# fox_rwkv7_hybrid_block on one core: the first branch weight cast on GpSimd, gate loads ahead of weight loads, modulation products singly between output products

## The chip, the cores and the metric

The kernel runs on one core of a Trainium2 chip. The metric is the device time of one execution in microseconds (us); the median of several runs is compared. One further execution was profiled, and every row of a profile comes from that one.

Engines go by the names of the profile: PE is TensorE's products and PEld its weight loads, DVE is VectorE, ACT is ScalarE, POOL is GpSimd, SP is SyncE. SPq is SP's queue, from which nearly all DMAs are issued, one behind the other.

## The reference

One block of a hybrid model over 1024 tokens of width 1024, all in float32. What is computed, cut to what matters:

```python
mod = silu(c) @ w_mod + b_mod
shift1, scale1, gate1, shift2, scale2, gate2 = split(mod, 6)
u = modulate(rms_norm(h, ln1_g), shift1, scale1)       # xn * (1 + scale) + shift
proj = u @ w_in                                         # fox columns, rwkv columns, gate columns
o_fox = fox_attention(q, k, v, log_sigmoid(f + b_f))    # 8 heads of 64
o_rwkv = rwkv7_time_mix(p_rwkv, ...)                    # 8 heads of 64
gate_fox, gate_rwkv = split(sigmoid(p_gate), 2)
merged = gate_fox * (o_fox @ fox_w_out) + gate_rwkv * (o_rwkv @ rwkv_w_out)
h = h + gate1 * (merged @ w_o)
u = modulate(rms_norm(h, ln2_g), shift2, scale2)
a, b = split(u @ w_up, 2)                               # 2816 columns each
h = h + gate2 * ((silu(conv(a)) * b) @ w_down)
out = rms_norm(h, final_g)
```

The change touches the products `o_fox @ fox_w_out` and `o_rwkv @ rwkv_w_out` (the branch products), `merged @ w_o` (the output product), and the two pieces shift2 and scale2 of `mod`.

## The kernel before

A float32 product is made of three products: each operand is split into a high part, rounded to the format that TensorE takes at full pace, and a low part, the remainder; high by high, low by high and high by low are summed in PSUM. A cast makes the high part, a subtraction the low part.

The order of TensorE's instructions is written out by hand. That of the other engines is, up to the middle of the output product, set by a scheduler that sees what each instruction needs, and by extra order edges (`add_manual_dep` with `NOSYNC`): such an edge says that one instruction stands behind another in the order, and adds no wait.

**Branch products.** `br_part(x, n, hf)` makes one part: branch x (0 attention, 1 RWKV), column tile n (0 to 7), token half hf. It has 12 products of 128x512 into one PSUM bank. 32 parts follow one another, in the order (0,0,0), (0,1,0), (0,0,1), (0,1,1), and then (x,n,0), (x,n,1) for each further n. They take banks 1 to 4 in turn, so that a part starts when VectorE has emptied the bank of the fourth part before it. VectorE does that with the multiplication by the gate: `mg = g * ps` for x = 0 (L1306), `g = g * ps` and `mg = mg + g` for x = 1 (L1308, L1309).

`br_open(x, n)` prepares a column tile. The raw weight `raw_br` is loaded by `br_load` (L1206, two buffers), ScalarE casts it into `hi_br` (L1214), GpSimd subtracts for `lo_br` (L1215), and the gate tile `g` is read back from DRAM (L1217, two buffers). Tile n+1 is opened, and the weight of tile n+2 loaded, ahead of the parts of tile n.

In the same stage run `mod_steps` (the loads `wm` of `w_mod`, L1267, and VectorE's sums over them into `acc`, for segments 3 and 4), `rk_make` (the RWKV operands: load `rk_raw`, ScalarE's cast, VectorE's subtraction, both into `rk_m` tiles, L1293 and L1294), `wo_load` (the weights of the output product) and `mg_split` (the split of the merged operand, tiles `mgh_f` and `mgl`). The work of the stage before ends beside the first parts: `fx` are the attention's operands, `tp` its transposes, `rk_ps` the last gate columns, `rest` their sigmoid.

**Output product.** `wo_mm(t, kt, ps)` makes six products of 128x512 for token tile t and contraction step kt. The loop goes over kt for t = 0 and 1, and from kt = 5 on steps of t = 2 follow. At kt == 4 the generator `mod_2` runs through: for each of the two segments eight fp32 products of a 128x128 piece of `acc` with a column of ones, into one column each of a PSUM tile `mps`; then VectorE adds the bias.

Of the kernel before, what the change touches and what calls it, by code (L numbers as in the profile page):

```python
# [17 lines left out]
KT = 8  # L18
NH = 512
# [16 lines left out]
NOSYNC = mybir.DependencyInfo(mybir.DependencyClass.NoSync, mybir.DependencyReason.DATA)  # L36
# [96 lines left out]
def hybrid_block(ctx: ExitStack, tc: tile.TileContext, a, out):  # L133
    nc = tc.nc
# [3 lines left out]
    def mm(o, lhsT, rhs, start, stop, more=False):  # L138

        weave.mm_cost(o, lhsT, rhs)  # L140
        nc.tensor.matmul(o, lhsT, rhs, start=start, stop=stop, skip_group_check=more)  # L141
# [5 lines left out]
    def f32(ap):  # L147
        return ap.bitcast(F32)
# [17 lines left out]
    def V(name, i=0, n=1):  # L166
        o, _ = VEC[name]
        return vec[:, o + i : o + i + n]
# [34 lines left out]
    d_gate = dr.tile([16, 128, S], F32, name="d_gate")  # L203
# [25 lines left out]
    def mod_part_steps(acc, ps, seg, dst):  # L229
        for j in range(KT):  # L230
            mm(ps[:, j : j + 1], acc[:, j * 128 : j * 128 + 128], ones[:, 0:1], start=True, stop=True)
            yield
        nc.vector.tensor_tensor(dst, ps[:, 0:KT], V("b_mod", seg * 8, KT), op=ALU.add)
# [10 lines left out]
    marks = {}  # L244
# [101 lines left out]
    with ExitStack() as es:  # L346
# [66 lines left out]
        with tc.tile_pool(name="st", bufs=1) as st, tc.tile_pool(name="stp", bufs=2, space=PS) as stp, \  # L413
# [126 lines left out]
            for half in range(2):  # L540
                for kt in u_steps(half):
                    low_part(kt, half, (0, 1))
                    if half == 0 and kt in (3, 5):
                        raw, hi, lo = low_raw[kt == 5]
# [465 lines left out]
    with tc.manual_schedule(engines={mybir.EngineType.DVE, mybir.EngineType.Activation}):  # L1010
# [6 lines left out]
        def slot(free):  # L1017
            while not free:
                yield 100
            yield free.popleft() - weave.now  # L1020
# [165 lines left out]
    def bank(k, name):  # L1186
        return pb.tile([128, NH], F32, tag="big", name=name) if k > 5 else pz.tile([128, NH], F32, tag=f"p{k}", name=name)
# [11 lines left out]
    br = br_st.enter_context(tc.tile_pool(name="br", bufs=2, reuse_waits="tile"))  # L1199
    opened = {}  # L1200

    br_raw = {}

    def br_load(x, n):
        raw = br_raw[x, n] = rp.tile([128, 1024], F32, tag="raw", name=f"raw_br{x}{n}")[:, 0:NH]
        nc.sync.dma_start(raw, a["w_br"][n, :, x * NH : x * NH + NH])  # L1206

    def br_open(x, n):
        if (x, n) not in br_raw:
            br_load(x, n)  # L1210
        raw = br_raw[x, n]
        hi = br.tile([128, NH], F32R, tag="whi", name=f"hi_br{x}{n}")
        lo = br.tile([128, NH], F32R, tag="wlo", name=f"lo_br{x}{n}")
        marks["br"] = nc.scalar.copy(hi, raw)  # L1214
        nc.gpsimd.tensor_tensor(lo, raw, f32(hi), op=ALU.subtract)  # L1215
        g = br.tile([128, S], F32, tag="g", name=f"g{x}_{n}")
        nc.sync.dma_start(g, d_gate[8 * x + n])  # L1217
        opened[x, n] = (hi, lo), g

    br_open(0, 0)  # L1220
    br_open(0, 1)
    if "rest" in marks:
        g, m = (gsp.tile([128, NH], F32, tag="sp0", name=f"rest{k}") for k in range(2))
        i = nc.scalar.activation(g, marks["rest"], AF.Abs)
# [36 lines left out]
    def mod_steps():  # L1261

        for seg in (3, 4):
            acc = slot(f"e{seg - 1}", f"acc{seg}")
            for kt in range(KT):
                w = slot(f"a{4 + kt % 4}", f"wm{seg}_{kt}")
                i = nc.sync.dma_start(w, a["w_mod"][kt * 128 : kt * 128 + 128, seg * D : seg * D + D])  # L1267
                if "i" in last:
                    tc.add_manual_dep(i.ins, last["i"].ins.name, NOSYNC)
                if kt == 0:  # L1270
                    ts(acc, w, sc[:, 0:1], None, op0=ALU.mult)
                else:
                    stt(acc, w, sc[:, kt : kt + 1], acc, op0=ALU.mult, op1=ALU.add)
                yield
            accs.append(acc)
# [8 lines left out]
    def mg_split(hf, n):  # L1284
        split(mg_hl[hf][0][n], mg_hl[hf][1][n], mg[hf][n])
# [24 lines left out]


    mods = mod_steps()
    for x in range(2):
        for n in range(8):
            if x or n:
                k = 8 * x + n + 1
                if k < 16:
                    br_open(k // 8, k % 8)
                if k < 15:
                    br_load((k + 1) // 8, (k + 1) % 8)  # L1320
            parts = [(x, n, 0), (x, n, 1)]
            if x == 0 and n < 2:
                parts = [(0, 0, 0), (0, 1, 0)] if n == 0 else [(0, 0, 1), (0, 1, 1)]
            for _ in range(0 if x and n > 3 else 1 if x else 2 if n < 6 else 0):
                next(mods, None)
            for part in parts:
                br_part(*part)
            if x == 0 and 1 <= n <= 4:
                rk_make((n - 1) // 2 * 2, (n - 1) % 2)
            if x == 1:  # L1330
                wo_load(n)
                if n == 0:
                    lo = [hp.tile([128, NH], F32R, tag=tag, name=f"mgl0_{k}", bufs=bufs)
                          for k, (tag, bufs) in enumerate(5 * [("xq", 5)] + 2 * [("s", 2)] + [("dg", 1)])]
                    mg_hl[0] = pairs([f"f{k}" for k in range(4)], "mgh0"), lo
                else:
                    mg_split(0, n - 1)
# [46 lines left out]
        h_sb[t] = slot(f"m{(4 if t < 4 else 8) + t}", f"h_sb{t}")  # L1384
        nc.sync.dma_start(h_sb[t], a["x"][t * 128 : t * 128 + 128, :])

    def wo_mm(t, kt, ps):
        hf, rows = t // 4, slice(t % 4 * 128, t % 4 * 128 + 128)
        x, w = [p[kt] for p in mg_hl[hf]], wo[kt]
        for c in range(2):  # L1390
            for n, (xi, wi) in enumerate(PARTS):
                mm(ps[c], x[xi][:, rows], w[wi][:, c * NH : c * NH + NH], start=kt == 0 and n == 0, stop=kt == KT - 1 and n == 2)

    def wo_row(t, ps):

        for c in range(2):
            cs = slice(c * NH, c * NH + NH)
            x, h = row_tmp[2 * t + c] if t < 5 else hp.tile([128, NH], F32, tag=("dg", "xq")[c], name=f"wo{t}_{c}", bufs=(1, 5)[c]), h_sb[t][:, cs]
            tt(x, ps[c], g1b[:, cs], op=ALU.mult)
            tt(h, h, x, op=ALU.add)  # L1400
            nc.scalar.activation(x, h, AF.Square, accum_out=ssq[:, 8 * c + t : 8 * c + t + 1])
        nc.sync.dma_start(d_h[t], h_sb[t])
# [213 lines left out]
    def mod_2():  # L1616
        for i, acc in enumerate(accs):
            yield from mod_part_steps(acc, bank(3 + i, f"mps{3 + i}"), 3 + i, m2[:, i * 8 : i * 8 + 8])
        stt(A2, m2[:, 8:16], 1.0, V("ln2_g", 0, 8), op0=ALU.add, op1=ALU.mult)
# [9 lines left out]

    ps = {t: [bank(k, f"wo{t}_{c}") for c, k in enumerate(ks)] for t, ks in enumerate(((0, 5), (6, 7), (1, 2)))}  # L1630
    behind = {5: (0, 1, 2, 3), 6: (4, 5), 7: (6, 7)}
    for kt in range(KT):
        for t in range(2):
            wo_mm(t, kt, ps[t])
        mg_split(1, kt)
        if kt == 4:
            for _ in mod_2():
                pass
        for k in behind.get(kt, ()):
            wo_mm(2, k, ps[2])  # L1640
    for t in range(3):
        wo_row(t, ps[t])
    def wo_do(t, k):
        ps = [bank(k + c, f"wo{t}_{c}") for c in range(2)]
        for kt in range(KT):
            wo_mm(t, kt, ps)
        return ps

    ps = wo_do(3, 3)
# [7 lines left out]
    ps = wo_do(4, 0)  # L1657
# [15 lines left out]
    for t, k in ((5, 2), (6, 6), (7, 4)):  # L1673
        ps = wo_do(t, k)
# [229 lines left out]
    for s, k in enumerate(ORDER):  # L1904
        ps = banks[4:] if k in (7, 4, 2) else banks[0:4]
# [109 lines left out]
```

## Time and profile before

| | |
|---|---|
| median of 3 runs | 1658.31 us (1658.08 to 1660.62) |
| the profiled execution's own time | 1662.01 us |
| span in its profile | 1660.2 us |
| mean granted TensorE clock | 0.989 |
| PE, PEld | 97%, 81% of the span |
| DVE, ACT, POOL | 74%, 50%, 8% |

The span is what the profile sees from the first instruction to the last; the execution's own time holds a little more. A share is an average over the whole span, and stages differ. The branch products lie at about 829 to 919 us, the output product behind them. In a row of the timeline stand start, length, engine, line, operation, output<-input and count, and in brackets the engine's idle time ahead of it and what ended that. L141 is the helper through which every product goes, so the tile's name tells products apart.

### The profile page before, as it was taken

What the parts mean: (1) busy time and instruction counts of PE and PEld (TensorE: products, weight loads), DVE (VectorE), ACT (ScalarE), POOL (GpSimd) and SP (SyncE); (2) the same over time, 40 slices, a digit from 0 to 9 for tenths busy, and PEclk for the clock granted to TensorE, in tenths of its full rate; (3) what the DMA queues carried; (4) which work ended last, traced back from release to release, by engine and by line L of the source; (5) the groups of instructions that cost most, each with busy time, mean ns of one, the idle gap of its engine ahead of it and who ended that gap; (6) DMA issues with size and microseconds to landing.
All of it is one profiled execution on the core that took longest, in us unless ns stands there. A gap on an engine that the chain in (4) does not pass through costs nothing.

```text
span 1660.2 us, 25947 instructions
## 1 busy us (share of the span) xinstructions
PE 1615.2 (97%) x9694; PEld 1346.1 (81%) x9694; DVE 1223.2 (74%) x2371; ACT 822.3 (50%) x1540; POOL 130.3 (8%) x152
## 2 busy tenths in 40 slices
PE   7999999999999999999999999999999999999998
PEld 7777777898978788888778887888888888888886
DVE  5786787878876536888678347897777777786677
ACT  5563335444455656666623225654444444555455
POOL 0011001111111011221022000000000000000000
PEclk9999999999999999999999999999999999999999
DMA  8488645443343246433187411243223223574363
GB/s 336 139 322 238 177 116 140 131 121 97 100 115 97 96 129 153 124 114 110 64 323 265 166 70 58 66 138 108 96 95 120 97 96 108 208 266 156 125 209 108
DMA packets 121645, 240.59 MB, mean 145 GB/s; under 512 B 40048, under 2 KB 48880, under 8 KB 121520
## 3 DMA queue, kind: packets, MB, share of 16 engines
q1 hardware_dynamic: 113040, 220.58, 40.7%
q0 software_dynamic: 8480, 18.37, 4.2%
q8 instruction: 76, 1.25, 0.3%
q14 instruction: 49, 0.40, 0.1%
HBM read 173.35 MB, written 65.54 MB: 144 GB/s over the span
## 4 chain that ended last, share of the span: by engine, by line
PE 62%; DVE 3%; ACT 2%; DMA 1%; issue 1%; SPq 0%; ACTq 0%; DVEq 0%
PE X L141 14%; PE D L141 13%; PE Y L141 7%; PE wo L141 5%; PE br L141 5%; PE gt L141 4%; PE rk_ps L141 4%; PE W L141 3%; PE lg L141 2%; PE ov L141 2%; PE tp L145 2%; DVE nm L1049 1%; DVE P L1059 1%; DMA g<-d_gate 0%; DVE tl L1089 0%
## 5 line engine op out<-in xcount | busy, mean ns | idle before, releaser
L141 PE MATMUL D<-op,op 128*128 128x512 f32 x924 | 209.8, 389 | 0.0
L141 PEld LDWEIGHTS D<-op,op 128*128 128x128 f32 x924 | 173.3, 188 | 36.3 <-DVE op L1252 0.3
L141 PE MATMUL X<-T_m,S 128*128 128x512 f32 x440 | 106.9, 389 | 0.0
L141 PEld LDWEIGHTS X<-T_m,S 128*128 128x128 f32 x440 | 82.5, 188 | 17.5 <-ACT x L1542 0.4
L1251 ACT CAST op<-g 128x512 fp32r<-128x512 f32 x77 | 47.8, 621 | 72.1 <-PE D L141 47.8
L1252 DVE TENSOR_TENSOR op<-g,op 128x512 fp32r<-128x512 f32 x77 | 53.0, 688 | 41.1 <-ACT op L1251 41.1
L1502 DVE SCALAR_TENSOR_TENSOR c<-ab,vec,c 128x512 f32<-128x512 f32 x88 | 65.9, 749 | 18.4 <-ACT c L1505 16.8
L784 DVE TENSOR_TENSOR t<-E,M 128x60 f32<-128x60 f32 (+24 forms) x248 | 56.1, 226 | 26.6 <-DMA M<-sm 20.6
L274 DVE TENSOR_TENSOR lo_in<-raw_in,hi_in 128x512 fp32r<-128x512 f32 x84 | 57.7, 725 | 22.0 <-PE gt L141 7.2
L1466 DVE TENSOR_TENSOR A<-ur,A 128x512 fp32r<-128x512 f32 x64 | 43.9, 688 | 39.0 <-ACT A L1462 38.8
L1466 DVE TENSOR_TENSOR S<-ur,S 128x512 fp32r<-128x512 f32 x66 | 45.5, 691 | 35.2 <-ACT S L1462 35.1
L1462 ACT CAST S<-ur 128x512 fp32r<-128x512 f32 x66 | 41.0, 622 | 56.1 <-DVE ur L1455 30.9
L141 PE MATMUL Y<-T_h,S 128*128 128x512 f32 x264 | 65.6, 398 | 1.6 <-ACT T_h L1720 1.0
L141 PE MATMUL Y<-T_h,A 128*128 128x512 f32 x264 | 63.4, 389 | 0.0
L1053 ACT ACTIVATE P<-lg,nm 128x896 f32<-128x896 f32 (+3 forms) x64 | 47.4, 742 | 29.3 <-DVE nm L1049 19.6
L141 PEld LDWEIGHTS Y<-T_h,S 128*128 128x128 f32 x264 | 50.6, 192 | 13.4 <-ACT T_h L1720 1.8
L1462 ACT CAST A<-ur 128x512 fp32r<-128x512 f32 x64 | 39.6, 621 | 42.9 <-PE X L141 31.0
L141 PE MATMUL W<-B_f,A 128*128 128x512 f32 x252 | 60.6, 389 | 0.0
L786 DVE TENSOR_TENSOR E<-E,t 128x60 f32<-128x60 f32 (+24 forms) x248 | 55.8, 225 | 6.4
L141 PE MATMUL X<-B_b,A 128*128 128x512 f32 x252 | 60.5, 389 | 0.0
L141 PEld LDWEIGHTS Y<-T_h,A 128*128 128x128 f32 x264 | 49.5, 188 | 10.3
L272 ACT CAST hi_in<-raw_in 128x1024 fp32r<-128x1024 f32 x42 | 43.9, 1049 | 25.4 <-PE ps_rkv L141 11.3
(481 smaller groups left out, 4142.0 us busy)
## 6 DMA issues: line engine op xcount, KB each, us to landing
raw_in<-in_w_in SPq DMA_DIRECT2D x50, 512.0 KB, 3.9
wm<-in_w_mod SPq DMA_DIRECT2D x48, 512.0 KB, 6.7
ur<-in_w_up SPq DMA_DIRECT2D x44, 512.0 KB, 4.0
g<-d_g SPq DMA_DIRECT2D x35, 512.0 KB, 3.8
d_g<-gs SPq DMA_DIRECT2D x44, 256.0 KB, 2.0
d_g<-c SPq DMA_DIRECT2D x33, 256.0 KB, 4.3
d_st<-qh SPq DMA_DIRECT2D x64, 128.0 KB, 2.4
stA<-d_st POOLq DMA_DIRECT2D x8, 1024.0 KB, 6.2
```

What stands on the lines that cost most here:

```text
L141: nc.tensor.matmul(o, lhsT, rhs, start=start, stop=stop, skip_group_check=more)
L145: nc.tensor.transpose(o, i, eye)
L272: nc.scalar.copy(hi, raw)
L274: nc.vector.tensor_tensor(lo[:, c : c + NH], raw[:, c : c + NH], f32(hi[:, c : c + NH]), op=ALU.subtract)
L784: tt(tv, E32[:, 0:J, s : s + 1].to_broadcast([128, J, W]), M32[:, s : s + 1, s + 1 : 32].to_broadcast([128, J, W]), op=ALU.mult)
L786: tt(E32[:, 0:J, s + 1 : 32], E32[:, 0:J, s + 1 : 32], tv, op=ALU.add)
L1053: nc.scalar.activation(e[:, 0:n], lg[:, 0:n], AF.Exp, bias=nm[:, 0:1], accum_out=nm[:, 1:2])
L1251: nc.scalar.copy(hi, src)
L1252: tt(lo, src, f32(hi), op=ALU.subtract)
L1462: nc.scalar.copy(hi, src)
L1466: tt(lo, src, f32(hi), op=ALU.subtract)
L1502: stt(c, ab[:, x + hf * NH : x + hf * NH + NH], V("conv_w", 22 * x + i), c, op0=ALU.mult, op1=ALU.add)
```

## The change

It has three parts.

1. The cast of the first weight (x = 0, n = 0) is done by GpSimd instead of ScalarE.
2. Each weight load of the branch products and each load `wm` gets an order edge to the gate load that was written last ahead of it in the code.
3. `wo_mm` takes a generator and draws one modulation product from it after every second product, for t = 0 and 1 from kt = 4 on; what is left is drawn at the last kt.

```diff
+    def after_gate(i):
+        if "g" in marks:
+            tc.add_manual_dep(i.ins, marks["g"].ins.name, NOSYNC)
+
     def br_load(x, n):
         raw = br_raw[x, n] = rp.tile([128, 1024], F32, tag="raw", name=f"raw_br{x}{n}")[:, 0:NH]
-        nc.sync.dma_start(raw, a["w_br"][n, :, x * NH : x * NH + NH])
+        after_gate(nc.sync.dma_start(raw, a["w_br"][n, :, x * NH : x * NH + NH]))
...
-        marks["br"] = nc.scalar.copy(hi, raw)
+        if x or n:
+            marks["br"] = nc.scalar.copy(hi, raw)
+        else:
+            nc.gpsimd.tensor_copy(hi, raw)
         nc.gpsimd.tensor_tensor(lo, raw, f32(hi), op=ALU.subtract)
         g = br.tile([128, S], F32, tag="g", name=f"g{x}_{n}")
-        nc.sync.dma_start(g, d_gate[8 * x + n])
+        marks["g"] = nc.sync.dma_start(g, d_gate[8 * x + n])
...
                 i = nc.sync.dma_start(w, a["w_mod"][kt * 128 : kt * 128 + 128, seg * D : seg * D + D])
+                after_gate(i)
...
-    def wo_mm(t, kt, ps):
+    def wo_mm(t, kt, ps, between=iter(())):
...
                 mm(ps[c], x[xi][:, rows], w[wi][:, c * NH : c * NH + NH], start=kt == 0 and n == 0, stop=kt == KT - 1 and n == 2)
+                if (3 * c + n) % 2:
+                    next(between, None)
...
+    mod2 = mod_2()
     for kt in range(KT):
         for t in range(2):
-            wo_mm(t, kt, ps[t])
+            wo_mm(t, kt, ps[t], mod2 if kt > 3 else iter(()))
         mg_split(1, kt)
-        if kt == 4:
-            for _ in mod_2():
+        if kt == KT - 1:
+            for _ in mod2:
                 pass
```

How this moves instructions shows at three places. The first is SP's queue at the start of the branch stage, before (`raw_br_9238` is the second weight, x = 0 and n = 1; `g_0` and `g_1` are the first two gate tiles; `d_gate<-gs` writes gate columns to DRAM):

```order
L1172 DMA d_gate<-gs_1_8654 128x512
L1206 DMA raw_br_9238<-in_w_br 128x512
L1172 DMA d_gate<-gs_0_8777 128x512
L1172 DMA d_gate<-gs_1_8940 128x512
L1172 DMA d_gate<-gs_0_9097 128x512
L1217 DMA g_0_9236<-d_gate 128x1024
L1217 DMA g_1_9244<-d_gate 128x1024
```

And the same place now:

```order
L1172 DMA d_gate<-gs_1_8654 128x512
L1172 DMA d_gate<-gs_0_8777 128x512
L1172 DMA d_gate<-gs_1_8940 128x512
L1172 DMA d_gate<-gs_0_9097 128x512
L1224 DMA g_0_9236<-d_gate 128x1024
L1210 DMA raw_br_9238<-in_w_br 128x512
L1224 DMA g_1_9244<-d_gate 128x1024
```

The second weight's load has moved behind three writes of gate columns and the first gate load. The second place is SP's queue further on, from the last write of gate columns, before (`raw_br_9372` and `raw_br_9420` are the weights of n = 4 and 5):

```order
L1231 DMA d_gate<-rest_9246 128x512
L1206 DMA raw_br_9372<-in_w_br 128x512
L1206 DMA raw_br_9420<-in_w_br 128x512
L1267 DMA wm_2_9326<-in_w_mod 128x1024
L1267 DMA wm_3_9329<-in_w_mod 128x1024
L1267 DMA wm_4_9374<-in_w_mod 128x1024
L1267 DMA wm_5_9377<-in_w_mod 128x1024
L1217 DMA g_2_9322<-d_gate 128x1024
L1217 DMA g_3_9370<-d_gate 128x1024
```

And now (`raw_br_9324` is the weight of n = 3, which stood ahead of this piece before):

```order
L1238 DMA d_gate<-rest_9246 128x512
L1224 DMA g_2_9322<-d_gate 128x1024
L1210 DMA raw_br_9324<-in_w_br 128x512
L1274 DMA wm_2_9326<-in_w_mod 128x1024
L1274 DMA wm_3_9329<-in_w_mod 128x1024
L1224 DMA g_3_9370<-d_gate 128x1024
L1210 DMA raw_br_9372<-in_w_br 128x512
L1274 DMA wm_4_9374<-in_w_mod 128x1024
L1274 DMA wm_5_9377<-in_w_mod 128x1024
L1224 DMA g_4_9418<-d_gate 128x1024
```

The gate tile of n = 2 has moved ahead of the weights of n = 3 to 5 and of four modulation weights, and from here on each weight stands right behind the gate tile of the column tile before it. The third place is TensorE's order in the output product, at the end of kt = 4 and the start of kt = 5 (`wo_0`, `wo_1` are the output product's banks, `wo_hi` and `wo_lo` the parts of its weight, `mgh_f` and `mgl` those of the merged operand, `acc_9281` and `acc_9470` the sums of segments 3 and 4), as a difference:

```order
+L141 MATMUL mps_10100<-cst,acc_9281 128x1
 L141 MATMUL wo_1_10039<-wo_hi_9871,mgl_4_9676 128x512
 L141 MATMUL wo_1_10039<-wo_lo_9872,mgh_f_9682 128x512
-L141 MATMUL mps_10112<-cst,acc_9281 128x1 x8
-L141 MATMUL mps_10122<-cst,acc_9470 128x1 x8
+L141 MATMUL mps_10100<-cst,acc_9281 128x1
 L141 MATMUL wo_0_10036<-wo_hi_9917,mgh_f_9682 128x512
 L141 MATMUL wo_0_10036<-wo_hi_9917,mgl_5_9677 128x512
+L141 MATMUL mps_10100<-cst,acc_9281 128x1
 L141 MATMUL wo_0_10036<-wo_lo_9918,mgh_f_9682 128x512
```

The block of sixteen products is gone from its place; six of them now lie in kt = 4, six in kt = 5 and four in kt = 6. On GpSimd the cast of the first weight stands where the subtraction for its low part stood, with that subtraction behind it; ScalarE's order has it no longer.

## The prediction

> **What bounds the kernel now.** I read the page first, for the share of each engine.
>
> ```profile
> span 1660.2 us, 25947 instructions
> PE 1615.2 (97%) x9694; PEld 1346.1 (81%) x9694; DVE 1223.2 (74%) x2371; ACT 822.3 (50%) x1540; POOL 130.3 (8%) x152
> ```
>
> TensorE (PE) is busy 97% of the span, so only two things can shorten the kernel: idle time of TensorE, and time in which it is busy at a poor rate. The chain of waits, in order of time, shows where the changed code stands in it.
>
> ```profile
> 829.09 10.30 PE br L141 x44
> ...
> 844.08 8.00 DMA g<-d_gate
> 853.01 65.69 PE br L141 x288
> 918.70 13.60 PE wo L141 x60
> 932.30 4.37 PE mps L141 x32
> 936.66 43.28 PE wo L141 x180
> ```
>
> The columns are start, length, engine, tile. The branch products (br) are interrupted once by a gate tile's load (g), and the output products (wo) once by the block of modulation products (mps). A branch part is 12 products: 65.69/24 = 2.74 us as the chain has it, 12 x 0.2267 = 2.72 at the output products' pace (13.60/60 = 0.2267 us). Three places can pay: TensorE's stall ahead of 829.09, its stall ahead of 853.01, and the mps block. The span is 1660.2, the profiled execution took 1662.01 (1.8 lie around the span), and the median of the runs is 1658.31, 3.7 below it. I take the saving from the profiled execution's own times and subtract it from the median. A measurement of this kernel can tell about 0.2%, 3.3 us, from no change.
>
> **Part 1, the first weight's cast on GpSimd (POOL).** The timeline around the first stall:
>
> ```profile
> 826.85 0.40 PE L141 MATMUL rk_ps<-u_hi,lo_in 128*128 128x512 f32 x1
> 827.89 0.62 ACT L1133 CAST fx<-o 128x512 fp32r<-128x512 f32 x1 [0.48 <-DVE o L1122]
> 828.42 1.14 ACT L1214 CAST hi_br<-raw_br 128x512 fp32r<-128x512 f32 x2
> 829.09 2.11 PE L141 MATMUL br<-fx,hi_br 128*128 128x512 f32 x8 [1.84 <-ACT hi_br L1214]
> 829.11 2.54 POOL L1215 TENSOR_TENSOR lo_br<-raw_br,hi_br 128x512 fp32r<-128x512 f32 x2 [46.79 <-DMA g<-d_gate]
> ```
>
> TensorE's first branch product waits for the cast hi_br, which stands on ScalarE (ACT) behind the cast of fx. That fx half belongs to the second token half, which the third part is the first to read. POOL had nothing to do for 46.79 us. The price of the cast on POOL, what it can wait for, and how long a weight takes to land:
>
> ```profile
> 780.21 0.61 POOL L1129 CAST fx<-o 128x512 fp32r<-128x512 f32 x1 [2.00 <-DVE o L1122]
> 823.98 0.49 PE L145 MATMUL tp<-cst,P 128*128 128x128 f32 x3
> 824.28 0.80 SPq L1217 DMA_DIRECT2D g<-d_gate  x2
> raw_br<-in_w_br SPq DMA_DIRECT2D x16, 256.0 KB, 3.8
> ```
>
> The cast's new tile lies in memory that the last transposes (tp, until 824.47) read, so it can run from 824.5 to 825.1, and the low part behind it is ready at about 825.1 + 2.54/2 = 826.4. Without the wait the first branch product starts one product after the last rk_ps: 826.85 + 0.23 = 827.08 for 829.09, **2.0 us earlier**. What is late next is the second weight. Its load now stands on SyncE's queue (SP) behind the gate load of 824.28, so it is issued at about 824.7, lands at 824.7 + 3.8 = 828.5, and its cast, on ScalarE behind fx, is ready at 829.0. The second part needs it at 827.08 + 2.72 = 829.80: 0.8 to spare. The term is bounded by 2.0 from above; from below a landing at the slowest that this tile shows in the trace (5.3) makes the second part 0.7 late, which leaves 1.3.
>
> **Part 2, gate loads ahead of weight loads.** The timeline around the second stall:
>
> ```profile
> 837.59 0.69 DVE L1306 TENSOR_TENSOR mg_m<-g,br 128x512 f32<-128x512 f32 x1 [1.84 <-PE br L141]
> 839.01 3.06 SPq L1206 DMA_DIRECT2D raw_br<-in_w_br  x2
> 840.92 3.75 DVE L1294 TENSOR_TENSOR rk_m<-rk_raw,rk_m 128x512 fp32r<-128x512 f32 x5
> 842.18 1.81 SPq L1267 DMA_DIRECT2D wm<-in_w_mod  x4
> 844.08 1.26 SPq L1217 DMA_DIRECT2D g<-d_gate  x2
> 848.14 1.88 DVE L1294 TENSOR_TENSOR rk_m<-rk_raw,rk_m 128x512 fp32r<-128x512 f32 x3
> 848.27 1.98 PE L141 MATMUL br<-fx,hi_br 128*128 128x512 f32 x8
> 852.18 1.28 DVE L1306 TENSOR_TENSOR mg_m<-g,br 128x512 f32<-128x512 f32 x2 [0.95 <-DMA g<-d_gate]
> 853.01 2.06 PE L141 MATMUL br<-fx,hi_br 128*128 128x512 f32 x8 [1.86 <-DVE mg_m L1306]
> g<-d_gate SPq DMA_DIRECT2D x16, 512.0 KB, 4.1
> ```
>
> The ninth part (853.01) takes the PSUM bank of the fifth, which VectorE (DVE) empties at 852.18 only because the gate tile of n=2 has just landed. That gate tile was issued at 844.08, behind two weights and four modulation weights (wm) on SP. The part before it starts at 848.27, so without the wait the ninth would start at 848.27 + 2.72 = 850.99 for 853.01: **2.0 us earlier**. In the new order g_2 is queued ahead of them. Its buffer is g_0's, which is free when VectorE has done the third part, 837.59 + 0.69 = 838.3, less the 2.0 of part 1: 836.3. It lands at 840.4. VectorE then has eight rk_m subtractions ahead of it (3.75 + 1.88 = 5.63 us, from 838.7), so the fifth part's product is through by about 845.0. Its bank is needed 2.0 earlier than now, at 849.0: 4 us to spare. The weight of n=3 pays for it, since it is queued behind g_2: issued 836.6, landed 840.4, cast 841.1, and needed at the seventh part, 827.08 + 6 x 2.72 = 843.4: 2.3 to spare, so it costs nothing up to a landing of 6.1. The bounds: all 2.0, or, with that landing at 5.3, still all 2.0; none of it if the gate load does not move up.
>
> The change ties every later weight load behind a gate load in the same way, and a gate load waits for VectorE. In the second branch VectorE is behind:
>
> ```profile
> 902.18 0.68 DVE L1309 TENSOR_TENSOR mg_m<-mg_m,g 128x512 f32<-128x512 f32 x1
> ```
>
> This is the add of the 24th part, whose products end at 853.01 + 16 x 2.74 = 896.8, so VectorE lags 6.1. From the end of that part to the first use of the weight that now waits for it lie four parts, 10.9 us. The lag (6.1), an issue (0.5), a landing (3.8) and a cast (0.7) make 11.1: 0.2 late, at a landing of 5.3 1.7 late. VectorE's lag shrinks by what TensorE waits, so this is paid about once and not for each weight. I take 0 here, since VectorE's lag ahead of this part is smaller, and keep 1.7 for the range.
>
> **Part 3, modulation products laid singly.** The stretches around the block, with PE busy and instructions, PEld, DVE, ACT, POOL, and then the granted clock; and the loads in it:
>
> ```profile
> 932.00:936.50 4.50, 4.50 (x34) 4.46 (x33) 0.17 (x1) 0.00 (x0) 0.00 (x0) 0.79 0.48 187
> 936.50:941.50 5.00, 5.00 (x13) 3.94 (x14) 0.33 (x2) 0.00 (x0) 0.00 (x0) 0.50 0.00 0
> 941.50:945.00 3.50, 3.50 (x17) 2.86 (x16) 0.00 (x0) 0.00 (x0) 0.00 (x0) 1.00 0.00 0
> 932.47 0.86 PEld L141 LDWEIGHTS mps<-cst,acc 128*128 128x128 f32 x7
> 677.55 0.39 PE L141 MATMUL lg<-stA 128*128 128x512 f32 x1
> 677.78 0.22 PE L141 MATMUL lg<-cst 128*128 128x128 f32 x1
> 677.84 0.45 PE L141 MATMUL lg<-stB 68*128 68x512 f32 x1
> 678.13 0.49 PE L145 MATMUL tp<-cst,P 128*128 128x128 f32 x3
> ```
>
> The block is 16 fp32 products of one column, in two passes each: 32 loads of 128x128 that stream next to nothing. It costs 4.37 us, and for the 5 us behind it the granted clock is 0.50, so the output products run there at about half their pace. From the chain, 4.37 + 43.28 = 47.65 us less 180 x 0.2267 = 40.80 is 6.85 us for the block and its dip. Singly, each product adds its passes between long ones. Seven loads in the block took 0.86 us at full clock; less 0.188 for the last, that is 0.112 a pass, 16 x 2 x 0.112 = 3.58. The attention stage has a short product between two long ones: from 677.55 to 678.13 is 0.58 for two long and one short, 0.58 - 0.454 = 0.126, 16 x 2 x 0.126 = 4.03. If the long neighbour hid one of the two loads, 16 x 0.126 = 2.0. I take 3.6 and no dip: 6.85 - 3.6 = **3.2 us saved**, between 4.8 and, with three loads exposed for each product (its two and the next long one's, 16 x 3 x 0.112 = 5.4), 1.45.
>
> The Trainium skill's page "TensorE: Matmul & The Clock Gate" (Part 3, "What overlaps and what doesn't") says that a weight load overlaps running products only where its row group differs; by that all three loads would be exposed and the total would be 1652.9. The pace of 0.2267 for long products whose loads use all 128 rows speaks against the rule.
>
> **The sum.** 2.0 + 2.0 + 3.2 = 7.2, taken as 7.3 unrounded (2.01 + 2.02 + 3.27). After 936.66 the chain is output products and then the FFN's products on TensorE, so the gain is kept. Span 1652.9, profiled execution 1654.7, median 1658.31 - 7.3 = **1651.0**.
>
> **The rivals.** *Loads exposed* (chance 0.09): the interleaving saves 1.45, 1651.0 + 1.85 = 1652.9. Against it stands the lg row, for it that no row shows an fp32 product with two passes there.
>
> *Weights late* (0.16): the second weight and one weight of the second branch land at 5.3, 0.7 + 1.7 = 2.4 late, 1653.4. For it speaks VectorE's lag, against it the median landing.
>
> *The clock falls wherever the products lie* (0.10, the slower side): 16 products lie between 36 long ones in three places, two close together and one later, and a long product with its share of a short one streams only two thirds of the time. If the gate counts that as too little, the 36 long ones run at 5.00/13 = 0.385, 0.16 more each, 5.7; the short ones' loads take twice as long, 3.6 more; each of two stretches needs a recovery as the one of now (43.28 - 40.80 = 2.5), 5.0. With 3.6 for the products that is 17.9 for 6.85 now: 11.0 worse, less the stalls' 4.0, **+7.0, 1665.3**. What I know of the gate's point in this trace:
>
> ```profile
> 677.00:680.40 3.40, 2.09 (x12) 1.00 1.13 261
> 680.40:683.80 3.40, 2.74 (x16) 0.74 0.32 84
> 700.80:704.20 3.40, 2.46 (x15) 1.00 0.51 138
> ```
>
> Here (PE alone, then clock) a stretch with 2.09 of 3.40 busy is followed by a fall to 0.74, one with 2.46 stays at 1.00. The new stretches leave TensorE no idle time at all, which is against the rival. The same page of the Trainium skill (Part 1, "A second HAM failure mode") tells of a kernel whose small idle spells between groups of products made the clock swing between half and full; that is this rival, and no row here shows it for spells as short as these.
>
> *The change does only part of it* (0.08): one of the stalls stays because the wait behind it ends as late as the one removed, and the products gain 1.45 or less: 1651.0 + 2.0 + 1.85 = 1654.9 or above, no change that can be told.
>
> **How the numbers follow.** Forecast 0.57 at 1651.0; the others as above. Low end: the best case of the products (4.8 for 3.27, 1649.5) and 1 us for what three runs leave open of the median, 1648.5. High end: exposed loads, late weights and half a stall together, 1651.0 + 1.85 + 2.4 + 1.2 = 1656.5; outside lies the clock rival. Faster by over 0.2% (below 1655.0): 0.57 + 0.09 + 0.13 of the late weights = 0.79; same 0.11, the rest of these; slower 0.10.
>
> **What would show it.** After: the first branch product within 0.3 us of the last rk_ps; no idle time over 0.3 ahead of the ninth part; a granted clock of 1.00 from the fifth output step on, with 180 long output products and the mps ones in about 40.8 + 3.6 = 44.4 us. Wrong if TensorE waits for hi_br or raw_br in the second branch, or if the clock falls twice.

## The result: 3.4 us less, half of what was forecast

| | before | changed |
|---|---|---|
| median of 17 runs each | 1658.31 us (1655.99 to 1664.01) | 1654.91 us (1653.05 to 1658.86) |
| profiled span | 1660.2 us | 1656.1 us |

The medians differ by 3.4 us. The ratio is 0.9979 with a 95% interval of 0.9971 to 0.9987: faster by 3.5 us, between 2.2 and 4.8. The forecast was 1651.0, 7.3 less. The measured time lies inside the range given (1648.5 to 1656.5), the sign was right, and the size was twice the measured one. The two profiled executions took 1662.01 and 1657.92 us, 3.7 and 3.0 more than the medians.

The timeline of TensorE in the changed kernel, at the first stall, at the places where it waits now, and at the ends of the stage (start, length, operation; in brackets the idle time and what ended it):

```profile
825.95 0.40 PE L141 MATMUL rk_ps<-u_hi,lo_in 128*128 128x512 f32 x1
826.18 2.02 PE L141 MATMUL br<-fx,hi_br 128*128 128x512 f32 x8
...
837.66 2.11 PE L141 MATMUL br<-fx,hi_br 128*128 128x512 f32 x8 [0.35 <-ACT hi_br L1219]
...
898.32 2.11 PE L141 MATMUL br<-rk_m,hi_br 128*128 128x512 f32 x8 [0.40 <-ACT hi_br L1219]
...
904.53 2.11 PE L141 MATMUL br<-rk_m,hi_br 128*128 128x512 f32 x8 [0.46 <-ACT hi_br L1219]
...
912.02 2.11 PE L141 MATMUL br<-rk_m,hi_br 128*128 128x512 f32 x8 [1.73 <-ACT hi_br L1219]
...
917.61 0.39 PE L141 MATMUL wo<-wo_hi,mgh_f 128*128 128x512 f32 x1
...
975.81 1.91 PE L145 MATMUL tr<-cst,h_sb 128*128 128x128 f32 x16
```

The first branch product now follows the last rk_ps product at 0.23 us: the first stall is gone. There is no wait ahead of the ninth part: the second stall is gone too. Instead TensorE waits four times for the high part of a weight, once in the first branch and three times in the second. In before the same stretch, from the first branch product to the first output product (918.53), took 918.53 - 829.09 = 89.44 us; here it takes 917.61 - 826.18 = 91.43. The stage gained the second stall (2.0) and is still 2.0 longer, so **4.0 us were lost in it**, as much as both stalls had cost.

The chain of waits of the changed kernel through the second branch says where from:

```profile
865.93 0.33 SPq L1224
866.25 0.05 issue
866.36 3.65 DMA raw_br<-in_w_br
...
872.22 5.17 DMA wm<-in_w_mod
877.41 0.04 DVE acc L1281
877.45 1.60 issue
879.05 0.69 DVE mg_m L1317
879.76 0.33 SPq L1224
880.09 0.04 issue
880.18 0.38 SPq L1210
880.56 0.05 issue
880.61 5.16 DMA wm<-in_w_mod
...
893.77 6.18 DMA wm<-in_w_mod
...
904.84 1.80 DVE mg_m L1317
906.65 0.33 SPq L1224
906.98 0.05 issue
907.07 4.18 DMA raw_br<-in_w_br
911.27 0.04 ACTq L1219
911.31 0.04 issue
911.35 0.63 ACT hi_br L1219
911.98 0.04 issue
912.02 5.76 PE br L141 x24
```

This is a ring. SyncE issues a gate load (L1224), and behind it, in this order, the next weight and a modulation weight (wm). VectorE's sum over wm (L1281) stands in VectorE's order ahead of the add (L1317) that frees the next gate buffer, and only that lets SyncE issue the next gate load, with the next weight and the next wm behind it. TensorE is not in the chain between 865 and 912. VectorE's own rows show the waits:

```profile
877.41 1.72 DVE L1281 SCALAR_TENSOR_TENSOR acc<-wm,sc,acc 128x1024 f32<-128x1024 f32 x1 [0.61 <-DMA wm<-in_w_mod]
885.80 1.73 DVE L1281 SCALAR_TENSOR_TENSOR acc<-wm,sc,acc 128x1024 f32<-128x1024 f32 x1 [1.68 <-DMA wm<-in_w_mod]
899.97 1.28 DVE L1281 SCALAR_TENSOR_TENSOR acc<-wm,sc,acc 128x1024 f32<-128x1024 f32 x1 [1.63 <-DMA wm<-in_w_mod]
```

These are 3.9 us of idle time on an engine that has next to none to spare here, and they end in the 1.73 us wait for the last weight at 912.02.

The output product went as forecast. Its stretches, in the columns of before (PE, PEld, DVE, ACT, POOL, then the granted clock), and one product in its place:

```profile
933.00:937.00 4.00, 4.00 (x25) 3.49 (x25) 0.17 (x1) 0.00 (x0) 0.00 (x0) 1.00 0.01 4
937.00:941.00 4.00, 4.00 (x19) 3.29 (x18) 0.00 (x0) 0.00 (x0) 0.00 (x0) 1.00 0.00 0
928.72 0.39 PE L141 MATMUL wo<-wo_hi,mgl 128*128 128x512 f32 x1
928.95 0.28 PE L141 MATMUL mps<-cst,acc 128*128 128x1 f32 x2
929.09 0.48 PE L141 MATMUL wo<-wo_lo,mgh_f 128*128 128x512 f32 x1
929.40 0.40 PE L141 MATMUL wo<-wo_hi,mgh_f 128*128 128x512 f32 x1
```

The clock stays at 1.00. From 928.72 to 929.40 are 0.68 us for two long products and one short: 0.23 for the short one's two passes, 0.115 a pass.

### The profile page after: what moved, and what is told of

It reads as the page before. It is cut to its first block, busy times and chain, and to the rows that moved or that the text cites. A ratio compares the mean times of both kernels' runs of the same rounds, so it can differ in the third digit from the quotient of the medians.

```text
span 1656.1 us, 25948 instructions
## 1 busy us (share of the span) xinstructions
PE 1609.8 (97%) x9694; PEld 1339.7 (81%) x9694; DVE 1221.6 (74%) x2371; ACT 822.3 (50%) x1539; POOL 129.8 (8%) x153
## 4 chain that ended last, share of the span: by engine, by line
PE 59%; DVE 4%; DMA 2%; ACT 2%; issue 1%; SPq 0%; POOL 0%; ACTq 0%; DVEq 0%
PE X L141 14%; PE D L141 13%; PE Y L141 7%; PE wo L141 5%; PE gt L141 4%; PE rk_ps L141 4%; PE W L141 3%; PE lg L141 2%; PE br L141 2%; PE ov L141 2%; PE tp L145 2%; DMA raw_br<-in_w_br 1%; DMA wm<-in_w_mod 1%; DVE nm L1049 1%; DVE P L1059 1%
```

## The experiments

In one execution the place of everything ahead of the branch stage varies by some us (the last rk_ps product starts between 824.1 and 828.7 in the runs below), so each kernel is compared by its time and by two stretches of its profile: the branch stage, from the first branch product to the first output product, and the output stage, from there to the transposes (tr) behind the third token tile. The whole is counted from the start of the last rk_ps product.

| kernel | branch stage | output stage | whole | ratio to before (95%) |
|---|---|---|---|---|
| before | 89.44 | 61.26 | 152.94 | |
| before, second profile | 89.91 | 58.04 | 150.19 | |
| before, third profile | 89.52 | 59.62 | 151.38 | |
| changed | 91.43 | 58.20 | 149.86 | 0.9979 (0.9971 to 0.9987) |
| changed, again | 89.38 | 58.20 | 147.82 | 0.9984 (0.9975 to 0.9993) |
| cast alone | 89.62 | 59.66 | 149.51 | 0.9991 (0.9980 to 1.0003) |
| order alone | 88.65 | 59.61 | 150.50 | 0.9998 (0.9985 to 1.0011) |
| singly alone | 89.38 | 58.19 | 149.81 | 0.9989 (0.9978 to 1.0000) |
| tied in the first branch alone | 87.65 | 58.19 | 146.08 | 0.9957 (0.9942 to 0.9973) |
| the same, again | 87.44 | 58.19 | 145.86 | 0.9976 (0.9964 to 0.9987) |
| only weights tied | 93.50 | 58.20 | 151.94 | 1.0011 (1.0001 to 1.0021) |
| only wm tied | 87.82 | 58.19 | 146.24 | 0.9967 (0.9955 to 0.9979) |
| without the last sums | 87.49 | 58.19 | 145.91 | one run |

**The three parts, each alone, and the ties in the first branch alone.** The cast alone is before with part 1 of the diff:

```diff
+        if x or n:
+            marks["br"] = nc.scalar.copy(hi, raw)
+        else:
+            nc.gpsimd.tensor_copy(hi, raw)
```

> The kernel before with the first part alone: the first weight is cast on GpSimd. Theory (the loss sits in the second branch, made by the tied loads; each other part pays what was worked out): the first branch product starts 0.25 us after the last rk_ps product instead of 2.2, and nothing else changes, so 2.0 us less than before, 1656.3. Rival 1 (what the first stall frees is eaten by the next wait, the late gate tile of n = 2): the gate load goes out when SyncE's queue comes to it, so the ninth part waits up to 2.0 longer and the time is that of before, 1658.3.

The first stall went (2.24 to 0.23 us from the last rk_ps product to the first branch product), and the second stayed, 1.50 us of idle time for the 1.86 of before:

```profile
849.88 2.08 PE L141 MATMUL br<-fx,hi_br 128*128 128x512 f32 x8 [1.50 <-DVE mg_m L1309]
```

The branch stage kept its length (89.62 for 89.44), so nothing was eaten: 2.0 us gained in the profile. The time says 1.5 us with an interval from 3.3 faster to 0.5 slower, which holds the theory's 2.0 and does not exclude the rival's 0; the profile does.

The order alone is before with `after_gate` on both kinds of load.

> The kernel before with the second part alone: gate loads ahead of weight loads and of modulation weights. Theory: the stall of 2.0 us ahead of the ninth part goes, and the second branch loses 3 to 4 us to weights and sums that come late, so 1 to 2 us more than before, 1659.3 to 1660.3, with waits of TensorE on hi_br in the second branch. Rival 1 (the losses in the second branch come from the earlier start, since it pulls VectorE's backlog together, and not from the tied loads): as for the stall alone, 2.0 less than before, 1656.3.

The time, 0.3 us less with an interval from 2.5 less to 1.8 more, holds both. In the profile both missed: the ninth part's stall of 2.0 went, and the stage got 0.8 shorter instead of 1 to 2 longer, so 1.2 us were lost in it. The ring was there, but weaker. VectorE waited 1.76 us for wm in the second branch (0.74, 0.85 and 0.17) for 3.92 in the changed kernel, and TensorE 0.68 for 2.59:

```profile
906.10 2.12 PE L141 MATMUL br<-rk_m,hi_br 128*128 128x512 f32 x8 [0.68 <-ACT hi_br L1218]
911.92 2.11 PE L141 MATMUL br<-rk_m,hi_br 128*128 128x512 f32 x8
```

Whether the earlier start of the changed kernel makes the ring's waits longer is not shown. Counted from the first product of the second branch, the gate loads of its first two column tiles go out 4.5 us before and 0.9 after it in both kernels, and VectorE has four sums over wm to come in both, so the two enter the second branch alike; and a second profile of the changed kernel, below, lies between this one and its first. That the earlier start is not the cause of the waits, as the rival has it, the kernel tied in the first branch alone shows.

Singly alone is before with the new `wo_mm` and loop.

> The kernel before with the third part alone: the modulation products lie singly between output products. Theory: 16 x 0.23 = 3.7 us for the products and no fall of the clock, 3.1 us less than before, 1655.2. Rival 1 (the dip of the clock only moves to a later place): no more than the products' own 4.4 - 3.7 = 0.7 us less, 1657.6.

The output stage took 58.19 us for 61.26, 3.07 less, and the clock did not fall; the dip did not move elsewhere. The time is only 1.8 us less (0 to 3.7); the profiles of before under "The clock's dip" below say why.

Tied in the first branch alone is the changed kernel with this condition:

```diff
-        if "g" in marks:
+        if "g" in marks and len(opened) < 8:
```

> The changed kernel, but weight loads and modulation weights are tied behind gate loads in the first branch alone; in the second their order is that of before. Theory: the second stall stays away and the second branch loses nothing, so what the changed kernel loses there (3.1 us of waits and 0.4 of refilling) comes back: 3 to 3.5 less than the changed kernel, 7 less than before, 1651.3. Rival 1 (the waits in the second branch come from the earlier start): the time of the changed kernel, 1654.9.

TensorE did not wait once from the second part to the end of the stage, as the chain of waits has it:

```profile
828.24 0.63 ACT hi_br L1219
828.87 0.04 issue
828.91 84.77 PE br L141 x372
```

The whole is 146.08 for 149.86, 3.8 less than the changed kernel, and the ratio 0.9957. The same start that the changed kernel has costs nothing here; the rival falls.

**Which tie makes the ring.** Three kernels take it apart. Only weights tied drops the tie of wm, only wm tied drops that of the weights, and the third leaves out the last four loads and sums of segment 4 while both ties stay.

```diff
-                after_gate(i)
```

> The changed kernel with only the branch weights tied behind gate loads; the modulation weights (wm) are free. They then stand one gate tile earlier in SyncE's queue. Theory (a ring in the second branch: gate load, behind it wm load, VectorE's sum over it, behind that the multiplication that frees the next gate buffer): the sums no longer hold VectorE up by more than 0.3 us, the gate loads come earlier, and the branch stage (first branch product to first output product) is 88 us for 91.4 in the changed kernel. Rival (a weight behind a gate load is enough by itself): 91 us, with TensorE's waits on hi_br in the second branch as before.

```diff
-        after_gate(nc.sync.dma_start(raw, a["w_br"][n, :, x * NH : x * NH + NH]))
+        nc.sync.dma_start(raw, a["w_br"][n, :, x * NH : x * NH + NH])
```

> The changed kernel with only the modulation weights (wm) tied behind gate loads; the branch weights are free. Theory (the ring goes through wm): VectorE still waits 1 to 1.7 us for wm in the second branch, gate loads still come late, but the weights do not, so TensorE waits only where VectorE's own lag reaches the bank of the fourth part before: branch stage 88 to 90 us. Rival (a weight behind a gate load is what does the harm, by itself): 87.6 us, that of the kernel tied in the first branch alone.

```diff
+                if seg == 4 and kt > 3:
+                    yield
+                    continue
                 w = slot(f"a{4 + kt % 4}", f"wm{seg}_{kt}")
```

> The changed kernel without the last four loads and sums of segment 4 (its output lacks them); weights stay tied behind gate loads everywhere. This takes the waiting sum out of the ring. Theory: no wait of VectorE on wm and none of TensorE on hi_br in the second branch, branch stage 87.6 to 88 us. Rival (a weight behind a gate load is enough by itself): the stage stays above 90 us. Four sums are 4 x 1.28 = 5.1 us of VectorE's work less, which alone could also let it catch up; the run with the weights tied alone keeps them and tells the two apart.

With only the weights tied the stage is 93.5, far from both numbers, and the kernel is slower than before by 0.11%. But its one wait lies in the first branch:

```profile
836.93 8.93 DMA raw_br<-in_w_br
...
845.96 0.63 ACT hi_br L1219
846.59 0.04 issue
846.63 3.65 PE br L141 x8
```

Four wm loads, free again, went out just ahead of g_2 and of the weight of n = 3, and that weight took 8.93 us to land: TensorE waited 4.00 us. In the second branch it did not wait at all, although each weight stands behind a gate load. It was close, though: the cast of the weight of n = 5 ended 0.09 us before its first product.

```profile
902.14 0.62 ACT L1219 CAST hi_br<-raw_br 128x512 fp32r<-128x512 f32 x1 [1.63 <-PE br L141]
902.85 2.07 PE L141 MATMUL br<-rk_m,hi_br 128*128 128x512 f32 x8
```

The row puts ScalarE's wait down to TensorE, but the weight, issued at 897.97 behind a gate load and landed 4.07 us later, came at 902.04, just ahead of the cast. In the kernel tied in the first branch alone the same cast has 4.7 to 5.5 us to spare. With only wm tied there was no wait in the second branch either (87.82), although VectorE waited 0.55 there for wm. Without the last sums the stage is 87.49, with both ties in place, but VectorE has 5.1 us less to do there. So neither tie made TensorE wait in the second branch by itself, and the rival that a weight behind a gate load is enough falls for these profiles, by 0.09 us; my theory's half that wm alone would cost up to 2 us falls with a stage of 87.82 beside 87.44 and 87.65.

What each tie does shows in the gate load ahead of the last weight, counted from the first product of the second branch, where all these kernels have the same four sums left (none in the last row):

| tied in the second branch | that gate load is issued after (us) | TensorE's idle time in that branch (us) |
|---|---|---|
| nothing (before; first branch alone, two profiles) | 32.4; 32.3, 32.8 | 0 |
| weights | 32.1 | 0 |
| wm | 33.9 | 0 |
| both (order alone; changed, two profiles) | 34.0; 36.2, 35.0 | 0.68; 2.59, 1.81 |
| both, without the last sums | 29.3 | 0 |

The tie of wm makes the gate load late, by 1 to 4 us, and the tie of the weights hands that lateness on to the next weight. **Both are needed** for a wait. The second, third and fifth lines of the table are one profile each.

**How far it repeats.** The changed kernel and the best one were run again on one chip.

> The changed kernel again, on the chip of the next run, to see how far its second branch repeats: theory (ring of gate load, wm landing and VectorE's sum): again three or four waits of TensorE on hi_br in the second branch, branch stage 90.5 to 92 us, 3 to 3.5 us less than before in time. Rival (the waits of the first profile were one execution's slow landings): branch stage below 89 us and the time about 6 us less than before.

The theory's three or four waits were one here, and its 90.5 was 89.38; VectorE waited for wm ahead of three of the four sums again (0.73, 1.51 and 0.47 us), and TensorE for the same last weight:

```profile
910.27 2.11 PE L141 MATMUL br<-rk_m,hi_br 128*128 128x512 f32 x8 [1.81 <-ACT hi_br L1219]
```

So the ring and the wait of 1.7 to 1.8 us at its end repeat; the two smaller waits ahead of it and the one in the first branch do not. The loss in the stage, against 87.4 to 87.7 without the ring, is 1.7 to 4.0 us. The rival's number (below 89) was missed too, by 0.4. This execution, 1656.29, lies 0.7 below its median, that of the first profile 3.0 above, so the smaller loss may be nearer to the usual one. The time, 0.9984, agrees with the first comparison.

> The kernel tied in the first branch alone, again, beside the changed kernel on one chip. Theory: branch stage 87.7 us, 7 us less than before and 3.5 less than the changed kernel. Rival (its gain came from the chip of that call): no more than the changed kernel's gain.

The stage is 87.44, again without a wait. The time is 4.0 us less than before (2.2 to 6.0), for 7.1 (4.5 to 9.6) in the first comparison; medians beside each other on one chip are 1655.03 and, for the changed kernel, 1656.97. It beats both kernels by its medians, and in the profile by 1.9 and 3.8 us against the changed kernel, but its interval overlaps with that kernel's (0.9975 to 0.9993). The medians on the one chip differ by 1.9, and drawing anew from the twelve times of each gives 0.5 to 3.7, so it leads, and by how much stays open.

**The clock's dip.** Before was profiled twice more, since the third part had saved 3.07 us in one profile and 1.8 in the time.

> The kernel before, profiled again, to see how far the terms of the sum repeat. Theory (the fall of the clock behind the block of modulation products lasts one or two windows of a clock that runs on its own, so its length is chance, and the stalls are not): both stalls of 2.0 us again, and 59.6 to 61.3 us from the first output product to the transposes behind the third token tile (58.2 without the block). Rival (the 61.3 of the first profile was the rule): within 0.2 of 61.3.

> The kernel before, profiled a third time, for the same question with the same expectations: 59.6 to 61.3 us for that stretch if the length of the dip is chance, within 0.2 of 61.3 if it is not; both stalls of 2.0 us in either case.

Both stalls were there again: 2.24 us from the last rk_ps product to the first branch product in both, and 2.30 and 1.88 us of idle time ahead of the ninth part, for 1.86 in the first profile. In the second profile the block of modulation products caused no dip. TensorE's rows there, and the granted clock of two stretches from the block on:

```profile
934.50 3.63 PE L141 MATMUL mps<-cst,acc 128*128 128x1 f32 x32
937.98 0.49 PE L141 MATMUL wo<-wo_hi,mgh_f 128*128 128x512 f32 x1
934.00:938.00 4.00, 4.00 (x36) 3.88 (x35) 0.17 (x1) 0.00 (x0) 0.00 (x0) 1.00 0.62 249
938.00:942.00 4.00, 4.00 (x20) 3.28 (x20) 0.34 (x2) 0.00 (x0) 0.00 (x0) 1.00 0.00 0
```

In the third it caused a short one:

```profile
936.00:941.00 5.00, 5.00 (x16) 3.95 (x15) 0.23 (x2) 0.00 (x0) 0.00 (x0) 0.66 0.00 0
```

With the block, the output stage took 61.26, 59.66, 59.61, 58.04 and 59.62 us in five profiles; singly, 58.19 or 58.20 in all eight. The lower bound of my theory (59.6) and the rival's 61.3 are both wrong. The third part saves 3.07, 1.4 or nothing, 1.4 on the mean of the five. The block is the same code in all of them; what decides between the three no run set.

## Why the prediction was right or wrong

**The first stall: right.** The cast on GpSimd took 0.61 us, as its row had it, and started at 823.64, 0.86 earlier than estimated in a run that was itself 0.9 earlier. The second weight's cast ended at 828.80 and was needed at 826.18 + 2.72 = 828.90: 0.1 to spare instead of 0.8, still in time.

**The second stall: right.** It is gone in every kernel that ties loads in the first branch; g_2 went out at 836.72 for 836.3, and VectorE came to the fifth part at 844.76, when it was to be nearly through (845.0); its bank was needed at 848.69. The weight of n = 2, which the prediction did not price, came late: it was issued at 827.34 (830.43 in before), right behind six loads of 512 KB, and took 9.55 us to land (4.24 in before; the prediction's slowest was 5.3). That cost 0.6 in one profile of the changed kernel and as much in the cast alone. In the other profile and in the kernel tied in the first branch alone the same weight took 8.5 to 9.0 and was just in time.

**The second branch, taken as 0: wrong, and the step that failed.** Against the 87.44 of a stage without the ring it measured 4.0 less the 0.6 in the first branch, 3.4 us, in the first profile, and 1.9 in the second. The forecast had nothing there. Three things in it were off. The prediction priced the tie of the weights and left that of wm uncosted, although it ties both; the ring needs both. It took a landing of 3.8 us for a weight, 5.3 at most; in the changed kernel the median was 4.9, and wm took 7.8. And it held that VectorE's lag shrinks by what TensorE waits, so that a delay is paid about once. In the second branch VectorE has nothing to make up with: in the kernel tied in the first branch alone, which has no ring, it is busy 41.24 of 44 us.

```profile
870.00:914.00 44.00, 44.00 (x196) 36.28 (x195) 41.24 (x49) 16.14 (x24) 11.25 (x7) 1.00 0.75 259
```

Each wait of VectorE for wm therefore moved every gate load after it, and TensorE paid three times, 0.40, 0.46 and 1.73 us of idle time. The rival "weights late" named the place and a price of 1.7 there; the measured price was up to twice that.

**The modulation products: mechanism right, size taken from one execution.** A pass cost 0.115 us for the estimated 0.112, the products 16 x 0.23 = 3.7 for 3.6, the clock stayed at 1.00, and the profile showed 3.06 us saved for 3.2. But the profile of before held the longest dip of five. The mean is 1.4, so this term was put 1.9 too high; the medians, 1.8 for this part alone (0 to 3.7), agree.

**The sum.** With the terms as the runs have them: 2.0 + 2.0 + 1.4 is 5.4, which is what the kernel tied in the first branch alone gained (4.0 and 7.1 in two comparisons, 5.5 by its two profiles against the three of before). Less 1.7 to 4.0 for the ring and the weight of n = 2 that leaves 1.4 to 3.7; 3.5 and 2.7 were measured.

The rival that the change does only part of it has the measured number, 1654.9, and that is luck: no stall stayed, and the products gained what their mechanism said; a new wait ate the gain. Of the other rivals, exposed loads fell: by the Trainium skill's page "TensorE: Matmul & The Clock Gate" (Part 3, "What overlaps and what doesn't") a product would have cost 0.336 (3 x 0.112, an estimate), and it cost 0.23, so one long product's load still lies under the products ahead of it. That the clock falls wherever the products lie fell as well: stretches with three short products for every six long ones kept 1.00.

## What to carry to other kernels

An order edge on a queue is a wait as soon as the instruction ahead of it can wait: before tying loads behind a load that waits for a buffer, follow who frees that buffer, and whether one of the tied loads is what that engine waits for; if so, the edge closes a ring, and here it cost what it did because that engine was nearly full. Tie loads only where the stall is (here the first branch), and leave the rest to the order that had slack. A cost that depends on the clock's window needs several profiles: one execution showed 3.1 us where five show 1.4.

## What the runs showed of the hardware

A busy TensorE can lose its clock, and in one and the same code it sometimes does and sometimes does not. After 3.6 to 4.4 us of one-column products the granted clock stayed at 1.00 in one of five profiles. From 932 to 946 us it averaged 0.76 in the first profile of before and 0.88 in the cast alone, the order alone and the third profile of before; with 0.50 as the low value that is 14 x 0.24 x 2 = 6.7 us at half pace in the one and 14 x 0.12 x 2 = 3.4 in the three. The Trainium skill's page "TensorE: Matmul & The Clock Gate" (Part 1, "What's actually happening") says that the gate watches a free-running window of about 3.4 us. The trace agrees: none, one or two such windows, and the lengths of the output stage, 58.0, 59.6 and 61.3, lie about 1.6 apart, where half of 3.4 is 1.7.

A weight of 256 KB landed in 3.8 us in the median of before. Right behind six loads of 512 KB it took 9.55 in the changed kernel, and 8.93 with only the weights tied, where four loads of wm and a gate load, 512 KB each, had just gone out ahead of it.
